# Weight split pieces queued behind every copy and split of the attention steps, value blocks ahead of prompt values, and other step lists for pairs 1, 6 and 7

## The chip, the cores and the metric

The kernel runs on one core of a Trainium2 chip. The metric is the device time of one execution in microseconds (us). The core has a matrix engine (PE, with its weight loads shown apart as PEld), a vector engine (DVE), a scalar engine (ACT), a general engine (POOL), and queues that issue DMAs (SP's above all). Each works through its own list of instructions in order and waits at semaphores for the others.

## The reference

The program is one inference step of a small trunk of two layers, on 512 frames of a new stream (the prompt) and 16 new frames each of 8 running streams (the sample), 640 columns in all, with 1024 features. Layer 0 is a convolution module and a feed-forward part (FFN). Layer 1 is the attention, with 16 heads of 64, and a second FFN. Everything is float32. The attention, where the change lies, is this (cut):

```python
k, v = jnp.split(rms_norm(h, norm_kv) @ w_kv, 2, axis=-1)
q = rms_norm(h, norm_attn[j]) @ w_q[j]
# prompt: each chunk of 64 frames sees itself and up to 8 chunks before it
s = jnp.einsum("bqhd,bkhd->bhqk", q_blk, k_blk) * scale + bias
p = jax.nn.softmax(jnp.where(valid, s, NEG_INF), axis=-1)
o = jnp.einsum("bhqk,bkhd->bqhd", p, v_blk)
# sample: 16 new frames see 512 cached rows and themselves, then the same softmax
h = h + o @ w_o[j]
```

## The kernel before

Every matrix product keeps float32 accuracy by splitting both factors into a high and a low part (`hi` a rounded copy made on ACT, `lo = x - hi` made on DVE) and adding three products: hi·hi, lo·hi, hi·lo. A weight set of 128x2048 comes by one DMA into `raw` and is split piece by piece into `whi` (ACT) and `wlo` (DVE). There are two buffers of each, so a set's pieces can be written once PE is done with the set two before it.

The attention stage works on **eight pairs of heads**, p = 0 to 7. For each pair the string `BO[p]` (L66 to L68) is a list of steps that sets PE's order by hand:

- `A`: the scores of the two prompt heads (`heads`, L1395, 24 matmuls that read `KH`, `KL`, `QH`, `QL`, into two wide PSUM tiles `w` and two narrow ones `am`), then bias and maximum on DVE (L1202), exponentials on ACT (L1194), scaling on DVE (L1428).
- `s0`, `s1`: the scores of the sample in two halves, into wide PSUM tiles, with their own maximum (`Sn`, `Ss`, L1202).
- `b00` to `b12`: transposes of the prompt's scores (L1441), copied to `PT` by ACT (L1445) or DVE (L1447).
- `t0`, `t1`: transposes of the sample's scores (L1491), copied to `PTs` by ACT (L1502); `n0`, `n1`: one more transpose each (L1497), copied to `PM` and `PN` by DVE (L1499).
- `P`: the prompt's values (`pair_c`, 16 matmuls, L1457); its result is split into `ohi` (ACT, L190) and `olo` (DVE, L192).
- `c0`, `c1`: the sample's values, 40 matmuls each (L1513); DVE scales each result (L1518). `d0`, `d1`: their transposes (L1522), split into `ohi` and `olo` in two parts each.
- `f` and a number: that many **fills**, or `f*`, all that the pair has left.

The `am` tiles have two buffers that are handed round in the order of the steps, so every `b`, `t`, `n`, `P`, `c` and `d` writes the buffer that the step but one before it used, and waits until that one's copy has been taken.

A **fill** is a portion of a projection (L1268) that is independent of the pair at work: one third of a product of the next keys and queries (`k`), of values (`v`), or one product of the attention's output projection (`o`). `SETS` lists the weight sets in order and `FILL[p]` how many fills a pair has. The keys and queries of pair p+1 are made by fills of pair p; a copy on ACT and a subtraction on DVE then turn them into `KH`, `KL`, `QH`, `QL` (`heads_split`, L1392 and L1393). An `o` fill ends in an addition to the residual `h` on DVE (L1357); after `s1` it uses half of a wide tile `w` where it can, and two products are then added at once.

While one weight set is used, the pieces of the next are issued, some at each fill (`pieces`, L1271). Where they stand in the lists of ACT and DVE is set by `past[-LAG]`: a piece is put behind the last **noted** instruction on each engine as it was four steps or fills ago (`note` records them in `ahead`). Noted are the copies to `PT`, the exponentials, the scalings, the `K`/`Q` splits and the additions that end fills; not noted are the copies to `PTs`, `PM` and `PN`, the scaling after `c`, and the splits after `P` and `d`.

After pair 7 a last projection (`halves`, L1527, matmuls at L202 to L204, additions at L1544) adds the rest of the attention to `h`; its weights are split whole (128x2048, L178 on ACT, L183 on DVE). The squares for the next norm follow (L1612), with the first weights of the second FFN (split at L374 and L375).

Of the kernel before, what the change touches and what calls it, by code (L numbers as in the profile page):

```python
# [8 lines left out]
F32 = mybir.dt.float32  # L9
# [55 lines left out]
          13 23 42 63 33"""  # L65
BO = ["A f4 s0 s1 f3 b00 f1 b01 f1 b02 f1 b10 f1 b11 f1 b12 f1 t0 f1 t1 f1 n0 n1 f1 P c0 c1 f2 d0 f1 d1 f*"] * 8  # L66
BO[1] = BO[6] = "A f4 s0 s1 f2 b00 f1 b01 b02 f1 b10 b11 f1 b12 t0 f1 t1 n0 n1 f1 P c0 c1 f1 d0 d1 f*"
BO[7] = "A f2 s0 s1 f4 b00 f1 b01 b02 f1 b10 b11 f1 b12 t0 f1 t1 n0 n1 f1 P c0 c1 f* d0 d1"  # L68
FILL = 27, 12, 28, 27, 28, 27, 16, 12
SETS = "k1 v1 k2 k3 o0 k4 v2 k5 o1 k6 v3 k7 o2"  # L70
LAG = 4
SSQ1 = 'aaaaaaaa'
# [13 lines left out]
def tile_trunk(ctx, tc, xT, vecs, hist, w_pw1, w_pw2, w_in0, w_out0, w_os0, w_in1, w_out1, w_os1,  # L86
# [102 lines left out]
    def xsplit(src, hi, lo):  # L189
        split_end[0] = nc.scalar.activation(out=hi, in_=src, func=AF.Copy).ins  # L190
        norm_end["xh"].append(split_end[0])
        nc.vector.tensor_tensor(out=lo, in0=src, in1=hi.bitcast(F32), op=ALU.subtract)  # L192

# [1012 lines left out]
    fill, step_end, spare_w2 = None, [None], [None, []]  # L1206
    ahead, past = {}, [{}] * LAG

    def note(ins):
        ahead[ins.ins.engine] = ins.ins  # L1210
        return ins

    def proj_kq(p):
# [126 lines left out]
    def set_o(r, w):  # L1340
        wh, wl = w
        for g0 in (0, NH):
            for m in range(KT):
                if spare_w2[0] and m % 2 == 0:
                    spare_w2[1] = [w2t().rearrange("p (a n) -> p a n", a=2)]
# [103 lines left out]
    def pair_c(p, PTs):  # L1449
        VT = vts[p // 2]  # L1450
        po = amt()
        for k in range(4):
            n = (4 - k) * P
            for hh in range(2):
                r = slice(hh * DH, hh * DH + DH)
                v0 = (p % 2) * P + hh * DH
                step_end[0] = nc.tensor.matmul(  # L1457
                    po[r, k * P:512], VT[:, 1 + k, v0:v0 + DH],
                    PTs[hh][:, POFF[k]:POFF[k] + n], start=(k == 0), stop=(k == 3)).ins
        xsplit(po, oT[p][0][:, P:], oT[p][1][:, P:])  # L1460

# [25 lines left out]
    def samp_b(u, S):  # L1487
# [7 lines left out]
        def rest():  # L1495
            tn = amt()
            step_end[0] = nc.tensor.transpose(tn[:, 0:P], S[:, 512 - v0:640 - v0], ident).ins  # L1497
            pn = PN if u else ap.tile([P, P], F32, tag="PM", name=nm("PM"), bufs=1)
            nc.vector.tensor_copy(pn[v0:, :], tn[v0:, 0:P])  # L1499
            return PT, pn  # L1500

        nc.scalar.activation(out=PT, in_=tr, func=AF.Copy)  # L1502
        return rest

    def samp_c(p, u, PTs, S, rs, VC):
# [4 lines left out]
        for k in range(5):  # L1510
            for b in range(4):
# [4 lines left out]
                    else VT[:, 0, (p % 2) * P:(p % 2) * P + P], start=k == 0, stop=k == 4).ins  # L1516
        os_ = S[:, 0:P]
        nc.vector.tensor_scalar(out=os_, in0=pv[:, 0:P], scalar1=rs[:, 0:1], scalar2=None,  # L1518
                                op0=ALU.mult)
        def rest():  # L1520
# [3 lines left out]
            for hh in range(2):  # L1524
                r = slice(hh * DH, hh * DH + DH)
                xsplit(trv[r, :, hh, :],
                       oT[p][0][r, v0:v0 + 64].rearrange("p (b q) -> p b q", q=SB),  # L1527
# [27 lines left out]
    for p in range(NP):  # L1555
# [3 lines left out]
        else:  # L1559
            oT[p] = (op_.tile([P, NT], F32, tag="kt", name=nm("ohi"), bufs=2).bitcast(F32R),  # L1560
                     op_.tile([P, NT], F32, tag="qt", name=nm("olo"), bufs=QB).bitcast(F32R))
        ha, sa, pt, ps, left = {}, {}, {}, {}, FILL[p]
        cache = [samp_load(p, u) for u in range(2)]
        for op in BO[p].split():
            if op[0] == "f":
                n = left if op[1] == "*" else min(left, int(op[1]))
                left -= n
                for _ in range(n):
                    with pe():
                        next(fill)  # L1570
                    past.append(dict(ahead))
                continue
# [258 lines left out]
```

## Time and profile before

| | |
|---|---|
| time, median of 3 runs (lowest to highest) | 1471.48 us (1471.44 to 1471.75) |
| the profiled execution: its own time, and its span | 1473.27 us, 1471.5 us |
| mean granted clock of PE | 0.992 |
| attention stage with all pairs, 693.5 to 1014.6 us | 321.1 us |
| busy in it: PE, DVE, ACT, POOL | 304.2, 190.9, 144.1, 46.4 us |

In rows of the profile, an instruction stands as line, engine, operation, what it writes, "<-", what it reads, and its shape. Behind an instruction, "[1.87 <-ACT PTs L1502]" says that its engine sat idle for 1.87 us before it, until ACT had written PTs at line 1502. Times at the left of a row are us from the start of the span; the time behind them is how long the row's instructions ran, several of one kind being merged ("x16").

### The profile page before, as it was taken

The numbers are of one execution on the slowest core, as the hardware profiler recorded it, in microseconds if no ns is written. First come the engines' busy times: TensorE is split into PE (matmuls) and PEld (weight loads), VectorE is DVE, ScalarE is ACT, GpSimd is POOL, SyncE is SP. The second block draws the span as 40 slices with busy tenths as digits, with TensorE's granted clock in tenths as the row PEclk, the third lists the DMA queues.
The fourth block names the chain that finished last, engine by engine and source line by source line (L and its number), as shares of the span: only waits on it lengthen the run. The fifth ranks groups of instructions, "written<-read, shape, count | busy, mean of one in ns | idle before, by whom it ended". The sixth has DMA issues, their size and how long they took to land. (4 is left out here: it accounts for less than half of the span.)

```text
span 1471.5 us, 28237 instructions
## 1 busy us (share of the span) xinstructions
PE 1433.5 (97%) x11086; PEld 1372.4 (93%) x11086; DVE 1117.9 (76%) x2486; ACT 748.9 (51%) x1633; POOL 282.3 (19%) x335
## 2 busy tenths in 40 slices
PE   9999999999999999999999999988999999999998
PEld 8998799999999999999877897877998999999998
DVE  6789867989788888666565656566899888888855
ACT  5666554554554554454544453433554455455443
POOL 5689120011110111012111111011001111111101
PEclk9999999999999999999999999999999999999999
DMA  7267434054544544415564464551224544544522
GB/s 241 77 180 184 120 86 143 18 136 142 136 105 146 134 105 132 125 58 207 183 205 152 143 208 149 164 185 37 79 76 130 140 119 119 150 118 107 157 63 72
DMA packets 66933, 192.58 MB, mean 131 GB/s; under 512 B 12144, under 2 KB 30320, under 8 KB 58480
## 3 DMA queue, kind: packets, MB, share of 16 engines
q1 hardware_dynamic: 52432, 160.58, 33.8%
q0 software_dynamic: 13504, 29.37, 10.0%
q8 instruction: 87, 1.43, 0.4%
q10 hardware_dynamic: 864, 0.83, 0.2%
q14 instruction: 46, 0.38, 0.1%
HBM read 179.14 MB, written 11.61 MB: 130 GB/s over the span
## 5 line engine op out<-in xcount | busy, mean ns | idle before, releaser
L442 PE MATMUL mm<-XH,whi 128*128 128x320 f32 x896 | 275.7, 310 | 2.6 <-ACT t L454 2.6
L442 PE MATMUL mm<-XH,wlo 128*128 128x320 f32 x896 | 276.1, 309 | 0.0
L442 PE MATMUL mm<-XL,whi 128*128 128x320 f32 x896 | 274.5, 309 | 0.0
L374 ACT ACTIVATE whi<-raw 128x512 fp32r<-128x512 f32 (+2 forms) x280 | 168.7, 613 | 142.3 <-PE mm L442 109.9
L375 DVE TENSOR_TENSOR wlo<-raw,whi 128x512 fp32r<-128x512 f32 (+2 forms) x280 | 185.4, 671 | 20.3 <-ACT whi L374 18.9
L442 PE MATMUL mm<-hid,whi 128*128 128x320 f32 x732 | 171.4, 310 | 2.7 <-DVE hid L375 2.3
L442 PEld LDWEIGHTS mm<-XH,whi 128*128 128x128 f32 x896 | 167.7, 188 | 4.2 <-ACT t L454 4.2
L442 PEld LDWEIGHTS mm<-XH,wlo 128*128 128x128 f32 x896 | 168.1, 188 | 0.0
L442 PEld LDWEIGHTS mm<-XL,whi 128*128 128x128 f32 x896 | 167.7, 188 | 0.0
L202 PE MATMUL mm<-xh,whi 128*128 128x320 f32 (+2 forms) x416 | 129.4, 313 | 0.8 <-DVE h L705 0.4
L442 PEld LDWEIGHTS mm<-hid,whi 128*128 128x128 f32 x732 | 124.8, 188 | 4.9 <-DVE hid L375 3.3
L203 PE MATMUL mm<-xh,wlo 128*128 128x320 f32 (+2 forms) x416 | 128.1, 310 | 0.0
L204 PE MATMUL mm<-xl,whi 128*128 128x320 f32 (+2 forms) x416 | 126.0, 310 | 0.0
L442 PE MATMUL mm<-hid,wlo 128*128 128x320 f32 x366 | 113.0, 309 | 0.0
L442 PE MATMUL mm<-XH,shi 128*128 128x320 f32 x344 | 105.9, 309 | 0.7 <-DVE h L1544 0.7
L442 PE MATMUL mm<-XH,slo 128*128 128x320 f32 x344 | 106.0, 308 | 0.0
L442 PE MATMUL mm<-XL,shi 128*128 128x320 f32 x344 | 105.5, 308 | 0.0
L844 POOL TENSOR_TENSOR ca<-ca,cvt 128x512 f32<-128x512 f32 x60 | 91.8, 1531 | 17.9 <-ACT cvt L841 11.3
L420 POOL DMA_DIRECT2D s<-in_w_in x38 | 22.0, 580 | 381.6 <-DVE wlo L375 150.6
L374 ACT ACTIVATE shi<-raw 128x512 fp32r<-128x512 f32 (+1 forms) x114 | 66.8, 588 | 43.0 <-PE mm L442 39.2
L583 DVE TENSOR_TENSOR h<-h,mm 128x320 f32<-128x320 f32 x168 | 80.5, 485 | 5.8 <-PE mm L442 5.6
L454 ACT ACTIVATE t<-mm 128x320 f32<-128x320 f32 x114 | 49.6, 435 | 66.0 <-PE mm L442 65.8
(331 smaller groups left out, 3728.6 us busy)
## 6 DMA issues: line engine op xcount, KB each, us to landing
raw<-in_w_in SPq DMA_DIRECT2D x38, 1024.0 KB
s<-in_w_in POOLq DMA_DIRECT2D x76, 256.0 KB, 4.1
raw<-in_w_os SPq DMA_DIRECT2D x24, 768.0 KB
cache<-in_ck SPq DMA_DIRECT2D x32, 512.0 KB
cache<-in_cv SPq DMA_DIRECT2D x32, 512.0 KB
raw<-in_w_pw SPq DMA_DIRECT2D x11, 1024.0 KB
s<-in_w_os POOLq DMA_DIRECT2D x48, 192.0 KB, 3.6
raw<-in_w_kq SPq DMA_DIRECT2D x8, 1024.0 KB
```

The source lines that it names most:

```text
L202: nc.tensor.matmul(ps, wh, xh, start=(first and i == 0), stop=False)
L203: nc.tensor.matmul(ps, wl, xh, start=False, stop=False)
L204: end = nc.tensor.matmul(ps, wh, xl, start=False, stop=(stop and i == last))
L374: put_end[1] = nc.scalar.activation(out=hi, in_=src, func=AF.Copy).ins
L375: put_end[0] = nc.vector.tensor_tensor(out=lo, in0=src, in1=hi.bitcast(F32), op=sub).ins
L420: nc.gpsimd.dma_start(s1, src[:, 2 * n:3 * n])
L442: last = nc.tensor.matmul(pt, wt, v, start=(first and k == i == 0), stop=(k == n - 1 and i == 2), skip_group_check=True)
L454: keeps.append(nc.scalar.activation(out=t, in_=pt, func=AF.Copy).ins)
L583: nc.vector.tensor_tensor(out=hv, in0=hv, in1=pt, op=sub if row else add)
L844: nc.gpsimd.tensor_tensor(out=acc, in0=acc, in1=pr, op=ALU.add)
```

## The change

Four things change, all in the attention stage.

- `LAG` goes from 4 to 1, and the copies to `PTs`, `PM`, `PN`, the scaling after `c`, and both halves of every split of `P` and `d` (the new helper `osplit`) are noted too. A weight piece thus stands behind everything that the last step put on its engine.
- In every list `c0 c1` now stand ahead of `P`. In pairs 0 and 2 to 5 a fill goes between `n0` and `n1` as well, and one fill fewer behind `P`.
- Pairs 1 and 6, which have 12 fills each now, end in `f1 n0 n1 c0 c1 P d0 d1` with no fill left; pair 7 has five fills behind `s1`, `P` behind `c1`, and its last fills between and behind `d0` and `d1`. `FILL` moves four `o` fills from pair 6 to pair 7.
- The last two `o` fills of a pair use the small `mm` tiles instead of a wide one (`left[0] > 2`), so that two additions of 128x320 take the place of one of 128x640.

```diff
-BO = ["A f4 s0 s1 f3 b00 f1 b01 f1 b02 f1 b10 f1 b11 f1 b12 f1 t0 f1 t1 f1 n0 n1 f1 P c0 c1 f2 d0 f1 d1 f*"] * 8
-BO[1] = BO[6] = "A f4 s0 s1 f2 b00 f1 b01 b02 f1 b10 b11 f1 b12 t0 f1 t1 n0 n1 f1 P c0 c1 f1 d0 d1 f*"
-BO[7] = "A f2 s0 s1 f4 b00 f1 b01 b02 f1 b10 b11 f1 b12 t0 f1 t1 n0 n1 f1 P c0 c1 f* d0 d1"
-FILL = 27, 12, 28, 27, 28, 27, 16, 12
+BO = ["A f4 s0 s1 f3 b00 f1 b01 f1 b02 f1 b10 f1 b11 f1 b12 f1 t0 f1 t1 f1 n0 f1 n1 f1 c0 c1 P f1 d0 f1 d1 f*"] * 8
+BO[1] = BO[6] = "A f4 s0 s1 f3 b00 f1 b01 b02 f1 b10 f1 b11 b12 f1 t0 t1 f1 n0 n1 c0 c1 P d0 d1 f*"
+BO[7] = "A f2 s0 s1 f5 b00 f1 b01 b02 f1 b10 f1 b11 b12 f1 t0 f1 t1 n0 n1 f1 c0 c1 P d0 f1 d1 f*"
+FILL = 27, 12, 28, 27, 28, 27, 12, 16
-LAG = 4
+LAG = 1
...
-        nc.vector.tensor_tensor(out=lo, in0=src, in1=hi.bitcast(F32), op=ALU.subtract)
+        return nc.vector.tensor_tensor(out=lo, in0=src, in1=hi.bitcast(F32), op=ALU.subtract)
...
+    def osplit(src, hi, lo):
+        note(xsplit(src, hi, lo))
+        ahead[split_end[0].engine] = split_end[0]
...
-                if spare_w2[0] and m % 2 == 0:
+                if spare_w2[0] and m % 2 == 0 and left[0] > 2:
...
-        xsplit(po, oT[p][0][:, P:], oT[p][1][:, P:])
+        osplit(po, oT[p][0][:, P:], oT[p][1][:, P:])
...
-            nc.vector.tensor_copy(pn[v0:, :], tn[v0:, 0:P])
+            note(nc.vector.tensor_copy(pn[v0:, :], tn[v0:, 0:P]))
...
-        nc.scalar.activation(out=PT, in_=tr, func=AF.Copy)
+        note(nc.scalar.activation(out=PT, in_=tr, func=AF.Copy))
...
-        nc.vector.tensor_scalar(out=os_, in0=pv[:, 0:P], scalar1=rs[:, 0:1], scalar2=None,
-                                op0=ALU.mult)
+        note(nc.vector.tensor_scalar(out=os_, in0=pv[:, 0:P], scalar1=rs[:, 0:1], scalar2=None,
+                                     op0=ALU.mult))
...
-                xsplit(trv[r, :, hh, :],
+                osplit(trv[r, :, hh, :],
...
-                n = left if op[1] == "*" else min(left, int(op[1]))
-                left -= n
-                for _ in range(n):
+                for _ in range(left[0] if op[1] == "*" else min(left[0], int(op[1]))):
                     with pe():
                         next(fill)
+                    left[0] -= 1
                     past.append(dict(ahead))
```

Three places show what the scheduler makes of it. The first is ACT's list in pair 2, from the copy of the prompt's transposes (`PT`) to the split behind `P` (`ohi` 128x512); `whi` is the set of keys and queries that is split in pieces. Before:

```order
L1392 ACTIVATE KH_9179<-kt_8967 128x512
L1445 ACTIVATE PT_8966<-am_9148 128x512
L1286 ACTIVATE whi_9199<-raw_9198,vec 128x128
L1392 ACTIVATE QH_9181<-qt_8968 128x512
L1286 ACTIVATE whi_9199<-raw_9198,vec 128x128 x13
L1502 ACTIVATE PTs_9209<-am_9204 128x512
L1286 ACTIVATE whi_9199<-raw_9198,vec 128x128 x2
L1502 ACTIVATE PTs_9225<-am_9220 128x512
L190 ACTIVATE ohi_8881<-am_9252 128x512
```

The same stretch of ACT's list in the changed kernel:

```order
L1396 ACTIVATE KH_9179<-kt_8967 128x512
L1449 ACTIVATE PT_8966<-am_9148 128x512
L1396 ACTIVATE QH_9181<-qt_8968 128x512
L1290 ACTIVATE whi_9199<-raw_9198,vec 128x128 x2
L1506 ACTIVATE PTs_9209<-am_9204 128x512
L1290 ACTIVATE whi_9199<-raw_9198,vec 128x128
L1506 ACTIVATE PTs_9225<-am_9220 128x512
L1290 ACTIVATE whi_9199<-raw_9198,vec 128x128 x3
L190 ACTIVATE ohi_8881<-am_9305 128x512
```

Two pieces instead of thirteen stand between `QH` and the first copy to `PTs`; the others have gone behind it, among and behind the splits of `P` and `d`. Pair 4 has the same.

The second place is DVE's list at the end of pair 6, where the weights of the last projection are split whole (`wlo` 128x2048). Before:

```order
L1499 COPY PM_11404<-am_11402 128x128
L1499 COPY PN<-am_11406 64x128
L192 TENSOR_TENSOR olo_11106<-am_11420,ohi_11105 128x512
L1518 TENSOR_SCALAR Sn<-am_11431,rs_11254 128x128
L1518 TENSOR_SCALAR Ss_11265<-am_11453,rs_11272 128x128
L1306 TENSOR_TENSOR qt_11192<-mm_11383,bc_7500 128x384
L1357 TENSOR_TENSOR h<-w_1323_11503,h 128x2x320
L183 TENSOR_TENSOR wlo_11860<-raw_11858,whi_11859 128x2048
L192 TENSOR_TENSOR olo_11106<-am_11491,ohi_11105 64x64
L192 TENSOR_TENSOR olo_11106<-am_11497,ohi_11105 64x64
L1393 TENSOR_TENSOR QL_11486<-qt_11192,QH_11485 128x512
L1357 TENSOR_TENSOR h<-w_1324_11517,h 128x2x320
```

The same stretch of DVE's list in the changed kernel:

```order
L1310 TENSOR_TENSOR qt_11196<-mm_11370,bc_7500 128x384
L1503 COPY PM_11435<-am_11433 128x128
L1503 COPY PN<-am_11437 64x128
L183 TENSOR_TENSOR wlo_11866<-raw_11864,whi_11865 128x2048
L1397 TENSOR_TENSOR QL_11428<-qt_11196,QH_11427 128x512
L1522 TENSOR_SCALAR Sn<-am_11440,rs_11258 128x128
L1522 TENSOR_SCALAR Ss_11269<-am_11462,rs_11276 128x128
L192 TENSOR_TENSOR olo_11110<-am_11484,ohi_11109 128x512
L192 TENSOR_TENSOR olo_11110<-am_11495,ohi_11109 64x64 x2
L192 TENSOR_TENSOR olo_11110<-am_11501,ohi_11109 64x64 x2
```

The whole subtraction has moved from behind the scaling after `c` to ahead of it, `qt` has moved ahead of `PM`, and no addition to `h` stands there any more. On ACT the whole copy to `whi` stands behind the two copies to `PTs` and ahead of `QH`.

The third place is ACT's list at the end of pair 7, with the splits behind `P` and `d` (`ohi`) and the first weights of the second FFN (`whi` 128x1024 and `shi`). Before:

```order
L1502 ACTIVATE PTs_11768<-am_11763 128x512
L190 ACTIVATE ohi_11531<-am_11784 128x512
L374 ACTIVATE whi_12057<-raw_12174 128x1024 x2
L190 ACTIVATE ohi_11531<-am_11846 64x64
L190 ACTIVATE ohi_11531<-am_11852 64x64
L190 ACTIVATE ohi_11531<-am_11846 64x64
L190 ACTIVATE ohi_11531<-am_11852 64x64
L374 ACTIVATE shi_12061<-raw_12103 128x512
```

The same stretch of ACT's list in the changed kernel:

```order
L1506 ACTIVATE PTs_11758<-am_11753 128x512
L190 ACTIVATE ohi_11507<-am_11818 128x512
L190 ACTIVATE ohi_11507<-am_11829 64x64 x2
L190 ACTIVATE ohi_11507<-am_11842 64x64 x2
L374 ACTIVATE shi_12067<-raw_12109 128x512
L374 ACTIVATE shi_12071<-raw_12109 128x512
L374 ACTIVATE shi_12069<-raw_12109 128x512
L374 ACTIVATE hid_12110<-raw_12109 128x512
L374 ACTIVATE whi_12063<-raw_12180 128x1024 x2
```

The two large copies have gone from ahead of the splits of `d` to behind them and behind the four smaller ones. At the beginning of pair 7, DVE's list has changed too: the maxima of the sample's scores (`Sn`, `Ss`) stand behind two additions to `h` and ahead of the scaling of the first head's scores, where they stood behind that scaling before. Outside the attention stage and the projection behind it (`halves`), the lists of all engines keep their order.

More of the change, by code (lines that the diff above doesn't have):

```diff
@@ L1206, in tile_trunk @@
     fill, step_end, spare_w2 = None, [None], [None, []]
-    ahead, past = {}, [{}] * LAG
+    ahead, past, left = {}, [{}] * LAG, [0]
     def note(ins):
@@ L1561, in tile_trunk @@
                      op_.tile([P, NT], F32, tag="qt", name=nm("olo"), bufs=QB).bitcast(F32R))
-        ha, sa, pt, ps, left = {}, {}, {}, {}, FILL[p]
+        ha, sa, pt, ps, left[0] = {}, {}, {}, {}, FILL[p]
         cache = [samp_load(p, u) for u in range(2)]
```

## The prediction

> **What bounds the kernel now.** I read the busy times first, then PE's waits, then the granted clock in windows of the attention stage, then PE, ACT and DVE side by side around each pause.
>
> The page, with the span and the busy time of each engine (us, share, instructions):
>
> ```profile
> span 1471.5 us, 28237 instructions
> PE 1433.5 (97%) x11086; PEld 1372.4 (93%) x11086; DVE 1117.9 (76%) x2486; ACT 748.9 (51%) x1633; POOL 282.3 (19%) x335
> ```
>
> PE is the bound: it works 97% of the span, and the change removes none of its matmuls. What can be won is PE's idle time and the time that it runs at a lower clock. PE's waits (line and tile <- what released it: us in total, times, longest) say where in the attention stage the idle time lies:
>
> ```profile
> PE am L1497 <- ACT PTs L1502: 4.3, 3, 1.9
> PE w L1412 <- DVE h L1357: 3.5, 3, 2.5
> ...
> PE mm L202 <- ACT ohi L190: 2.6, 1, 2.6
> ...
> PE w L1268 <- DVE mx L1202: 1.9, 1, 1.9
> ...
> PE am L1513 <- DVE olo L192: 1.6, 8, 0.3
> PE am L1497 <- DVE PM L1499: 1.5, 4, 0.4
> ...
> PE w L1412 <- ACT QH L1392: 1.1, 1, 1.1
> ```
>
> These seven rows hold 16.5 us. None of them names the pieces `whi` or `wlo` of a weight set, so weights arrive in time today.
>
> A pause costs more than itself when the clock falls after it. The windows (us; busy PE, PEld, DVE, ACT, POOL; then the granted clock PEclk, the DMA share and GB/s):
>
> ```profile
> 766.72:770.14 3.42, 2.10 (x20) 1.48 (x19) 2.85 (x9) 2.42 (x8) 0.00 (x0) 1.00 0.94 334
> 794.03:797.44 3.41, 1.78 (x10) 1.28 (x12) 0.80 (x3) 2.25 (x7) 0.00 (x0) 1.00 0.00 0
> 797.44:800.86 3.42, 3.42 (x14) 1.34 (x12) 1.40 (x4) 0.00 (x0) 0.00 (x0) 0.50 0.00 0
> 882.78:886.19 3.41, 1.74 (x10) 1.28 (x12) 0.76 (x3) 2.29 (x7) 0.00 (x0) 1.00 0.01 2
> 978.35:981.76 3.41, 0.90 (x7) 0.54 (x8) 3.10 (x7) 0.35 (x2) 0.00 (x0) 1.00 0.71 220
> 992.00:995.42 3.42, 3.42 (x14) 3.42 (x14) 2.06 (x11) 1.63 (x4) 1.24 (x2) 0.50 0.28 41
> 1014.60:1027.05 12.45, 11.47 (x67) 11.21 (x67) 10.14 (x25) 5.80 (x12) 0.00 (x0) 0.86 0.01 1
> 693.51:1014.60 321.09, 304.22 (x2824) 266.27 (x2823) 190.87 (x606) 144.10 (x413) 46.42 (x81) 0.98 0.52 166
> ```
>
> In 794.03 to 797.44 PE is busy for 1.78 us, and in the 3.42 us behind it the granted clock is 0.50: half of 3.42, 1.7 us of work, is lost. The windows from 882.78 (1.74 busy) and 978.35 (0.90) stand ahead of two more half-clock stretches. The one from 766.72, with 2.10 busy, was followed by none. So a stretch at half clock comes, in this trace, where PE was busy for about 1.8 us or less of 3.4. The whole attention stage lasts 321.09 us with PE busy 304.22: 17 us is the most that pauses alone can give there.
>
> **Pairs 2 and 4: the pieces ahead of `PTs`.** ACT's timeline (start, us, what it did) and PE's:
>
> ```profile
> 790.84 3.89 ACT L1286 ACTIVATE whi<-raw,vec 128x128 fp32r<-128x128 f32 x13
> ```
>
> PE beside it, in pair 2:
>
> ```profile
> 795.27 0.33 PE L1497 MATMUL am<-ident,Sn 128*128 128x128 f32 x1 [1.87 <-ACT PTs L1502]
> ...
> 797.12 4.07 PE L1457 MATMUL am<-PT,vt 128*64 128x512 f32 x16
> ```
>
> and `P` of pair 1, at full clock:
>
> ```profile
> 760.38 2.38 PE L1457 MATMUL am<-PT,vt 128*64 128x512 f32 x16
> ```
>
> Thirteen pieces take 3.89 us, 0.30 each, and `n0` waits 1.87 us for the copy behind them. With two pieces there (0.6 us), the copy comes 11 x 0.30 = 3.3 us sooner, so that wait goes. What is late next is `n1`, which waited 0.38 (the row on `PM` with four waits and 0.4 the longest); the fill now between `n0` and `n1` covers it. So 2.25 us in each of the two pairs: **4.5**. The 4.07 of `P` against 2.38 in pair 1 is the half clock: 1.7 each, **3.4**. In pairs 1 and 6 the other two of the four waits on `PM` go as well, **0.7**, as a fill separates `t1` from `n0`.
>
> **The copies and splits between steps.** PE's timeline at pair 1's end and at the scores (`A`) of pairs 2 and 3, and ACT's split of `P`:
>
> ```profile
> 764.17 1.08 PE L1513 MATMUL am<-cache,PTs 128*32 128x128 f32 x32 [0.19 <-DVE olo L192]
> ...
> 768.03 0.50 PE L1412 MATMUL w<-KH,QH 64*128 64x512 f32 x2 [1.09 <-ACT QH L1392]
> ...
> 771.01 0.38 PE L1268 MATMUL mm<-xh,whi 128*128 128x256 f32 x1
> ```
>
> PE at `A` of pair 3:
>
> ```profile
> 815.80 0.50 PE L1412 MATMUL w<-KH,QH 64*128 64x512 f32 x1 [0.48 <-DVE h L1357]
> ...
> 817.93 0.39 PE L1268 MATMUL mm<-xh,whi 128*128 128x256 f32 x1
> ```
>
> ACT behind `P` of pair 1:
>
> ```profile
> 762.80 0.60 ACT L190 ACTIVATE ohi<-am 128x512 fp32r<-128x512 f32 x1 [4.14 <-PE am L1457]
> ```
>
> - `c1` waited for `P`'s split in all eight pairs, 1.6 by its row. With `c0 c1` ahead of `P` it doesn't: **1.6**.
> - `A` of pair 2 starts 1.09 late and takes 771.01 - 768.03 = 2.98, where `A` of pair 3 takes 817.93 - 815.80 = 2.13. Pair 1's queries are now finished five steps sooner, so 1.09 + 0.85 = **1.9** goes.
> - `A` of pairs 3 and 5 wait 0.48 each for a 640-wide addition to `h`. The last two additions are now of single tiles and no longer hold a wide one: **1.0**.
>
> Against these stands what the lists of pairs 1 and 6 add. DVE around the end of pair 6:
>
> ```profile
> 965.92 0.29 DVE L1499 COPY PM<-am 128x128 f32<-128x128 f32 x1 [0.84 <-PE am L1497]
> ...
> 974.49 0.56 DVE L1306 TENSOR_TENSOR qt<-mm,bc 128x384 f32<-128x384 f32 x1 [0.86 <-PE mm L1268]
> ...
> 977.21 2.28 DVE L183 TENSOR_TENSOR wlo<-raw,whi 128x2048 fp32r<-128x2048 f32 x1
> ...
> 979.67 0.68 DVE L1393 TENSOR_TENSOR QL<-qt,QH 128x512 fp32r<-128x512 f32 x1
> 980.27 0.81 DVE L1357 TENSOR_TENSOR h<-w,h 128x640 f32<-128x640 f32 x1
> ```
>
> ACT there:
>
> ```profile
> 974.48 1.91 ACT L178 ACTIVATE whi<-raw 128x2048 fp32r<-128x2048 f32 x1 [3.36 <-PE mm L1268]
> ```
>
> - `c0` writes the `am` buffer of `n0` and waits until `PM` is copied. The fill just ahead of `n0` is the last of the queries, and its `qt` (0.56) now stands ahead of `PM` (0.29) on DVE: 0.85 in each of pairs 1 and 6, **1.7** added. No bound is below zero, since nothing is taken away there; if `qt` starts a fill earlier than I think, it is 0.
> - `d1` writes the buffer of `P`, and only `d0`, two transposes, stands between them. In pair 1 of before, `P` ended at 760.38 + 2.38 = 762.76, `ohi` followed at 762.80, and the waiting `c1` started at 764.17: 1.4 us. Less 0.1 for `d0` that is 1.3, twice: **2.6** added. The cover that is gone is `c0`.
> - In pair 6 `P` writes `c0`'s buffer, and so waits for the scaling of `c0`. On DVE `PM`, `PN`, the 2.28 of `wlo` and the 0.68 of `QL` stand ahead of that scaling, and `wlo` needs `whi`, which takes 1.91 on ACT from the second `PTs` on. From there DVE is free after 1.91 + 2.28 + 0.68 + 0.3 = 5.2 us, while PE has `n0`, `n1`, `c0` and `c1`, about 0.8 + 2 x 1.1 = 3.0: it waits **2.2**. By the windows above such a gap halves the clock, 1.7 more: **3.9** added. Behind the waiting `P` stand `d0`, `d1` and `A` of pair 7. Its ends: 0, if the copy to `whi` finds ACT free much sooner, and 5.2.
>
> **Pair 7 and the end.** PE's waits:
>
> ```profile
> 981.13 0.50 PE L1412 MATMUL w<-KH,QH 64*128 64x512 f32 x1 [2.51 <-DVE h L1357]
> ...
> 984.44 0.63 PE L1268 MATMUL mm<-ohi,whi 128*128 128x320 f32 x1
> ...
> 991.80 0.48 PE L1268 MATMUL w<-ohi,whi 128*128 128x320 f32 x1 [1.87 <-DVE mx L1202]
> ...
> 1014.60 0.42 PE L202 MATMUL mm<-ohi,whi 128*128 128x320 f32 x1 [2.61 <-ACT ohi L190]
> ```
>
> DVE ahead of the fill at 991.80, and ACT ahead of the end:
>
> ```profile
> 989.80 1.27 DVE L1428 TENSOR_SCALAR S<-S,rs 128x512 f32<-128x512 f32 x4
> 990.99 0.75 DVE L1202 CUSTOM_DVE_ANT_0 Sn<-w,BS 128x576 f32<-128x576 f32 x1
> ```
> ```profile
> 1011.80 2.00 ACT L374 ACTIVATE whi<-raw 128x1024 fp32r<-128x1024 f32 x2 [3.25 <-PE w L1268]
> ```
>
> - `A` waited 2.51 for an addition (980.27) that stood behind `wlo`, and took 3.31 instead of 2.13 at the lower clock. No addition is left there: 2.51 + 1.18 = **3.7** goes.
> - The first wide fill behind `s1` waited 1.87 for the sample's maximum, and the window from 992.00 ran at half clock. The maximum has moved ahead of the scaling (1.27), which leaves 0.6, but behind two additions of at most 0.81 each: 0.6 to 2.2, of which I take **1.2**, as one addition has time to finish beside `s1`. Then 1.87 + 1.7 = **3.6** goes and 1.2 comes back.
> - At the end the two copies of 2.00 us stood ahead of `ohi`, and PE waited 2.61. They now stand behind it. The window from 1014.60 lost (1 - 0.86) x 12.45 = 1.7 by the clock, but DVE was busy 10.14 of its 12.45, so I count 1.2 of it: 2.61 + 1.2 = **3.8** goes.
> - `d1` and the finer alternation of fills and steps in pair 7 and the other lists: **1.0** added, between 0 and 2, by the 0.29 of such a copy a few times.
>
> **The weights.** Every piece now stands later, and LAG 1 gives it the last place that is possible. I cost that at nothing. Its cover is a whole weight set: pieces are issued while the set before is used, and no wait row names one now. The rival below says what it costs without the cover.
>
> **The sum.** Removed: 4.5 + 3.4 + 0.7 + 1.6 + 1.9 + 1.0 + 3.7 + 3.6 + 3.8 = 24.2. Added: 1.7 + 2.6 + 3.9 + 1.2 + 1.0 = 10.4. Net 13.8 faster. The sum is made against the span of 1471.5; the profiled execution's own time, 1473.27, has 1.8 us around the span, and the median without a profile, 1471.48, happens to equal the span, so I take the sum off that: **1457.7 us**.
>
> The Trainium skill, "TensorE: Matmul & The Clock Gate", section "Why this matters for your kernels", weighs a clock loss only for idle gaps longer than about 3 us. The trace differs: a 1.87 us gap, in a window with 1.78 us of work, was followed by a clock of 0.50. By the page, the wait of pair 6 would cost no clock.
>
> **The rivals.**
>
> - *The waits return elsewhere, with the clock.* The pauses that I price without the clock in pairs 1, 6 and 7 (0.85 and 1.3 us close together, 1.2 in pair 7) each fill a window with under 1.8 us of work, three more stretches of 1.7: 5.1 back, **1462.8**. For it: 1.87 us was enough. Against it: the window from 766.72 with 2.10 busy was not. Chance 0.23.
> - *The new waits are hidden.* The copy to `whi` in pair 6 may start sooner and `qt` be done: 1.7 + 3.9 + 2.6 of the added terms fall away, **1449.5**. Against it: the buffers follow the order strictly. Chance 0.13.
> - *A gap of 2.2 us doesn't halve the clock.* Pair 6 then costs 2.2, and the time is **1456.0**. Against it: the window from 794.03. Chance 0.04. (This is what the rule of the Trainium skill's "TensorE: Matmul & The Clock Gate" would give; on the gaps that this trace shows, it doesn't hold.)
> - *Slower: weights come late.* Where a set ends, PE waits for the next set's last piece: 0.30 on ACT, 0.36 on DVE for the low part (by 2.28 to 1.91), and a copy of 0.6 ahead of it make 1.25, and the half clock 1.7 more: 2.9 at each of 12 set borders, 35 us, **1493**. It decides against the change from 13.8 / 12 = 1.15 us a border. Against it: no wait row names a piece today, and the order shows most of a set's pieces well ahead of its first use. Chance 0.05.
> - *Nothing comes of it.* The pauses may be set by something that the moved rows only hide, such as the transfers of the caches. Against it: ACT's rows end exactly where PE's waits do. Chance 0.05, at **1471**.
>
> **How the numbers follow.** The forecast, 1453 to 1462, has 0.50. The range takes in the hidden waits and the returned ones: 1448 to 1466, which leaves out the two cases at the end and the edges, under 2 in 10. A measurement of this kernel can tell about 0.2% (2.9 us) from no change. Faster: 0.50 + 0.23 + 0.13 + 0.04, and a little for a weaker form of late weights, 0.91; slower 0.05; the same 0.04.
>
> **What would show it.** Right: no row of `n0` waiting for `PTs` in pairs 2 and 4; `P` of pairs 2 to 5 at 2.4 us; `c1` without waits on `olo`; `A` of pair 7 at once; `ohi` at the end ahead of the copies for the FFN; in pair 6 a wait of `P` for the scaling of `c0` of about 2.2 us, with one stretch at half clock; pauses of 1.3 at `d1` of pairs 1 and 6. Wrong: PE waits that name `whi` or `wlo`; half-clock stretches in pairs 1, 6 and 7 beyond that one; a wide fill of pair 7 that still waits 2 us.

## The result, and the profile after

| | before | changed |
|---|---|---|
| time, median (lowest to highest) | 1471.62 us (1471.44 to 1472.6, 4 runs) | 1452.14 us (1451.49 to 1454.72, 4 runs) |
| ratio to before | | 0.987, 95% interval 0.9852 to 0.9887 |
| the profiled execution's own time | 1473.27 us | 1452.18 us |
| its mean granted clock | 0.992 | 0.999 |

The changed kernel is 19.5 us faster, 1.3%. The forecast was 13.8 us faster, 1457.7, in a range from 1448 to 1466.

The page of the changed kernel, its span and its busy times:

```profile
span 1450.3 us, 28244 instructions
PE 1420.6 (98%) x11086; PEld 1365.9 (94%) x11086; DVE 1119.6 (77%) x2489; ACT 749.7 (52%) x1633; POOL 283.0 (20%) x335
```

PE has the same 11086 matmuls and is busy 12.9 us less. At most 8.5 of this comes from the clock in the attention stage (the windows below); part of the rest is matmuls that ran alone ahead of a wait and counted as busy there (the rows under "What a wait costs"), which no run sizes as a whole. DVE and ACT do what they did. PE's waits in the stages that the change touches (line and tile <- releaser: us in total, times, longest):

```profile
PE am L1526 <- DVE olo L192: 2.7, 3, 1.2
PE am L1461 <- DVE Sn L1522: 2.1, 1, 2.1
...
PE am L1517 <- DVE PM L1503: 1.2, 2, 0.6
PE w L1622 <- DVE sqs L1615: 1.0, 1, 1.0
...
PE w L1272 <- DVE mx L1202: 0.8, 1, 0.8
...
PE am L1501 <- ACT PTs L1506: 0.6, 1, 0.6
```

Of the seven rows shown of before (16.5 us) two are left, `mx` with 0.8 for 1.9 and `PTs` with 0.6 for 4.3. Three have come in their place, and each is one that the prediction adds: `d1` for the split of `P` (L1526), `P` of pair 6 for the scaling of `c0` (L1461), and `c0` for `PM` (L1517). The wait for `sqs` was there before, with the same 1.0.

To see where the time went, the attention stage is cut at each pair's first matmul of the scores, from PE's timeline, and ended at the first product of the second FFN. Each entry is the difference of two such starts, in us:

| from A of pair | before | changed | difference |
|---|---|---|---|
| 0 to A of pair 1 | 44.77 | 44.27 | -0.5 |
| 1 to 2 | 29.74 | 29.49 | -0.3 |
| 2 to 3 | 46.79 | 41.20 | -5.6 |
| 3 to 4 | 42.90 | 41.42 | -1.5 |
| 4 to 5 | 45.90 | 41.17 | -4.7 |
| 5 to 6 | 42.90 | 41.42 | -1.5 |
| 6 to 7 (four fills fewer now) | 31.60 | 31.25 | -0.4 |
| 7 to the FFN (four more) | 54.50 | 46.71 | -7.8 |

Together 339.1 against 316.9, 22.2 us less. The windows of the whole stage, of before (us; busy PE, PEld, DVE, ACT, POOL; granted clock, DMA share, GB/s):

```profile
693.51:1032.62 339.11, 320.99 (x2925) 282.34 (x2924) 205.95 (x637) 150.85 (x427) 48.15 (x82) 0.97 0.50 161
```

and of the changed kernel:

```profile
694.92:1011.84 316.92, 308.24 (x2925) 276.26 (x2925) 207.53 (x640) 151.54 (x427) 48.19 (x82) 1.00 0.53 172
```

The granted clock went from 0.97 to 1.00: before, five stretches of 3.41 us at 0.50 lay in it, which cost at most 5 x 1.7 = 8.5 us of PE's work; now there is none. The other 13.7 us or more are waits, counted from one start to the next. The stage moved by 22.2 and the profiled execution by 1473.27 - 1452.18 = 21.1, because the changed kernel reached the stage 1.4 us later in it; single executions of one kernel differ by more (1451.49 to 1454.72 here).

In pair 2 the thirteen pieces ahead of `PTs` have become two. ACT's timeline there in the changed kernel:

```profile
790.62 0.68 ACT L1290 ACTIVATE whi<-raw,vec 128x128 fp32r<-128x128 f32 x2
791.21 0.58 ACT L1506 ACTIVATE PTs<-am 128x512 f32<-128x512 f32 x1
...
792.33 0.60 ACT L1506 ACTIVATE PTs<-am 128x512 f32<-128x512 f32 x1 [0.26 <-PE am L1495]
```

PE beside it:

```profile
793.02 0.27 PE L1501 MATMUL am<-ident,Sn 128*128 128x128 f32 x1
794.00 0.27 PE L1501 MATMUL am<-ident,Ss 128*128 128x128 f32 x1
795.08 1.08 PE L1517 MATMUL am<-cache,PTs 128*32 128x128 f32 x32
...
797.40 2.37 PE L1461 MATMUL am<-PT,vt 128*64 128x512 f32 x15
```

The second copy to `PTs` now waits for PE, and PE no longer waits for the copies; `n0`, `n1` and `c0` show no idle time, and `P` takes 2.37 where it took 4.07.

At the end of pair 6 the waits forecast have come. DVE's timeline:

```profile
955.80 0.56 DVE L1310 TENSOR_TENSOR qt<-mm,bc 128x384 f32<-128x384 f32 x1 [2.36 <-PE mm L1272]
956.28 0.28 DVE L1503 COPY PM<-am 128x128 f32<-128x128 f32 x1
...
957.75 2.29 DVE L183 TENSOR_TENSOR wlo<-raw,whi 128x2048 fp32r<-128x2048 f32 x1 [0.86 <-ACT whi L178]
959.96 0.69 DVE L1397 TENSOR_TENSOR QL<-qt,QH 128x512 fp32r<-128x512 f32 x1
960.67 0.35 DVE L1522 TENSOR_SCALAR Sn<-am,rs 128x128 f32<-128x128 f32 x1
```

PE's:

```profile
956.61 1.08 PE L1517 MATMUL am<-cache,PTs 128*32 128x128 f32 x32 [0.63 <-DVE PM L1503]
...
961.08 2.37 PE L1461 MATMUL am<-PT,vt 128*64 128x512 f32 x16 [2.08 <-DVE Sn L1522]
963.38 0.33 PE L1526 MATMUL am<-ident,Sn 128*128 128x128 f32 x1
964.88 0.33 PE L1526 MATMUL am<-ident,Ss 128*128 128x128 f32 x1 [1.16 <-DVE olo L192]
```

`c0` waits behind `qt` and `PM`, `P` behind `wlo` and `QL`, and `d1` for the split of `P`, one after the other as they stand in the lists. But `P` takes 2.37: no half clock follows.

### The profile page after: what moved, and what is told of

Its sections match the earlier page's. It is cut to its first block, busy times and chain, and to the rows that moved or that the text cites. A ratio compares the mean times of both kernels' runs of the same rounds, so it can differ in the third digit from the quotient of the medians.

```text
span 1450.3 us, 28244 instructions
## 1 busy us (share of the span) xinstructions
PE 1420.6 (98%) x11086; PEld 1365.9 (94%) x11086; DVE 1119.6 (77%) x2489; ACT 749.7 (52%) x1633; POOL 283.0 (20%) x335
## 3 DMA queue, kind: packets, MB, share of 16 engines
q0 software_dynamic: 13504, 29.37, 10.2%
## 5 line engine op out<-in xcount | busy, mean ns | idle before, releaser
L844 POOL TENSOR_TENSOR ca<-ca,cvt 128x512 f32<-128x512 f32 x60 | 92.0, 1533 | 17.7 <-ACT cvt L841 11.2
```

What stands on the lines that cost most here:

```text
L844: nc.gpsimd.tensor_tensor(out=acc, in0=acc, in1=pr, op=ALU.add)
```

## The experiments

The runs of the kernel before that are named with a job's medians were taken on the same chip as that job's kernels.

**One half at a time.** The pieces alone: the changed kernel with the lists (`BO`), `FILL` and tiles of before, so that only the place of the pieces is new.

```diff
-FILL = 27, 12, 28, 27, 28, 27, 12, 16
+FILL = 27, 12, 28, 27, 28, 27, 16, 12
...
-                if spare_w2[0] and m % 2 == 0 and left[0] > 2:
+                if spare_w2[0] and m % 2 == 0:
```

> Only the place of the weight pieces changes (LAG 1 and the added notes); lists, FILL and the tiles of the last fills are those of before. Theory (the parts add up): n0 of pairs 2 and 4 no longer waits for PTs, 2 x 2.6 us by start to start, and P there runs at full clock, 2 x 1.7: about 8.6 us less, 1463; the waits of c1 on olo (8 x 0.2), of A in pairs 3, 5 and 7 and the 2.6 us at the end stay. Rival (the pieces' gain needs the new lists, since pieces now stand ahead of the split of P or of d): c1 or d waits longer than before in pairs 2 and 4, and under 4 us is left, 1467.5 or more.

The lists alone: the changed kernel with `LAG` and the noted instructions of before.

```diff
-LAG = 1
+LAG = 4
...
-        osplit(po, oT[p][0][:, P:], oT[p][1][:, P:])
+        xsplit(po, oT[p][0][:, P:], oT[p][1][:, P:])
...
-        note(nc.scalar.activation(out=PT, in_=tr, func=AF.Copy))
+        nc.scalar.activation(out=PT, in_=tr, func=AF.Copy)
```

> The new lists, FILL and the tiles of the last fills, with LAG 4 and without the added notes. Theory (the parts add up): the 8.6 us of pairs 2 and 4 are missing from the changed kernel's gain of 19.5, so 1460 to 1461; n0 of pairs 2 and 4 waits about 1.9 us for PTs behind 13 pieces, with a half-clock stretch behind it, while c1 has no waits on olo and the end has ohi ahead of the FFN copies. Rival (lists alone let pieces stand ahead of P's split as well): over 1464.

Measured beside 1472.23 for the kernel before: pieces alone 1462.09 (ratio 0.9938, interval 0.9914 to 0.9961), lists alone 1461.76 (0.9933, 0.9919 to 0.9948), both changes 1450.61 in the same job (0.9856, 0.9841 to 0.9871). The halves give 10.1 and 10.5, together 20.6, and the whole 21.6: in sum the parts add up. With the pieces alone, pairs 2 and 4 last 42.04 and 41.50 us instead of 46.79 and 45.90. The other pairs keep their times within 0.2, but for two: the stretch from pair 7 to the FFN lasts 52.61 instead of 54.50, and pair 3 lasts 43.76 instead of 42.90 because a transpose waits for `PT` behind pieces that now stand later:

```profile
827.68 0.44 PE L1445 MATMUL am<-ident,S 128*128 128x128 f32 x2 [0.63 <-ACT PT L1449]
```

That price is absent in the whole change, whose list has other fills there.

Place by place the halves do not add up so simply. With the lists alone, pairs 2 and 4 last 3.5 and 2.0 us longer than in the changed kernel, 5.6 together where 8.6 was expected, and the stretch from pair 7 to the FFN lasts 52.37 instead of 46.71, 5.7 longer, which neither expected text has. With the lists alone, DVE's list has the first head's scaling ahead of the sample's maximum again, and PE waits for that maximum, with two windows at half clock behind it:

```profile
981.16 0.64 PE L1272 MATMUL w<-ohi,whi 128*128 128x320 f32 x1 [3.79 <-DVE mx L1202]
```

So about half of what the pieces add to the lists is won in pair 7, by another order of DVE's list, and not at `PTs`.

The lists alone showed something else, too. Pair 2 lasts 44.71 us there and pair 4 only 43.21, with the same pieces ahead of the same copy. Windows of that kernel, each pair's pause and the 3.41 us behind it:

```profile
792.42:795.83 3.41, 1.54 (x13) 1.28 (x11) 1.29 (x4) 3.41 (x12) 0.00 (x0) 1.00 0.04 13
795.83:799.24 3.41, 3.41 (x18) 3.04 (x20) 2.02 (x5) 0.69 (x2) 0.00 (x0) 0.50 0.00 0
877.75:881.16 3.41, 2.00 (x15) 1.73 (x13) 2.06 (x6) 3.41 (x13) 0.00 (x0) 1.00 0.10 35
881.16:884.58 3.42, 2.96 (x46) 2.76 (x50) 1.94 (x5) 1.47 (x4) 0.00 (x0) 1.00 0.00 0
```

In pair 2 the pause fell into one window, with 1.54 busy, and half clock followed. In pair 4 it fell across two, with 2.00 and 2.96 busy, and none followed. The half-clock stretches of every execution lie on a grid of 3.41 us, and where the grid lies against the program differs between executions. So one and the same pause costs up to 1.7 us more or doesn't, by chance; here the pairs differ by 44.71 - 43.21 = 1.5.

**Does the wait of `P` in pair 6 lower the clock?** The changed kernel, again:

> The changed kernel unaltered, for another execution in the profile. Theory (the clock is granted anew on a grid of 3.41 us that is fixed within one execution and differs from one to the next; a window with under about 1.8 us of PE work is followed by one at 0.50): the wait of P in pair 6, 2.1 us long, is again there, and a stretch at 0.50 follows in this profile if, and only if, one window of this execution's grid holds 1.6 us or more of PE's idle time there; single times scatter between 1451.5 and 1455. Rival (a gap of 2.1 us never lowers the clock): no stretch in the attention stage in any execution, times within 0.5 us.

It ran at 1450.61 (1450.11 to 1451.61), with the same wait of 2.08 and no stretch at half clock in the attention stage. Its grid cut the pause in two (PE was still busy 1.97 us in the emptier window), so this alone tells nothing. It was looked at again in the last job:

> The changed kernel unaltered once more, beside the next one: 1450 to 1453, and the attention stage, from A of pair 0 to the first product of the second FFN, at 316.9 us if the wait of P in pair 6 is followed by no stretch at half clock, 318.6 if it is.

It ran at 1451.51 (1451.23 to 1452.43), beside 1471.1 for the kernel before, the stage at 316.9 once more. Here the grid did hold the pause. Windows of this execution, the pause and what follows:

```profile
959.00:962.42 3.42, 1.52 (x8) 0.63 (x10) 2.07 (x4) 0.00 (x0) 0.00 (x0) 1.00 0.87 280
962.42:965.83 3.41, 2.25 (x20) 1.45 (x18) 1.27 (x5) 1.35 (x5) 0.00 (x0) 1.00 0.90 297
```

With 1.52 us busy, less than in pair 2 of before (1.78), no half clock follows. The condition that I expected, that PE's busy time in a window of the grid decides, failed here; the experiment below without `left[0] > 2` holds another such window. The matmuls that fill the window differ: here it is half of `P`, there products of fills and two transposes. Two experiments further down have windows that fit no bound on busy time either: the first two lines are the kernel before with `c0 c1` ahead of `P`, where 1.76 us, all of it products of the last projection, keep the clock; the last two are the weights of the last projection in pieces, where 2.33 us, with six one-column products of the squares among them, lose it:

```profile
1004.83:1008.24 3.41, 1.76 (x12) 1.76 (x13) 0.71 (x4) 3.21 (x9) 0.00 (x0) 1.00 0.00 0
1008.24:1011.65 3.41, 3.41 (x25) 3.41 (x24) 3.40 (x8) 2.23 (x5) 0.00 (x0) 1.00 0.02 5
1001.89:1005.31 3.42, 2.33 (x18) 2.14 (x17) 3.10 (x8) 0.00 (x0) 0.96 (x1) 1.00 0.16 19
1005.31:1008.72 3.41, 3.41 (x15) 3.10 (x14) 2.39 (x5) 0.44 (x1) 0.77 (x1) 0.50 0.99 334
```

So the pause was made longer. First the scaling of `c0` was done five times over:

```diff
+        if p == 6 and not u:
+            for _ in range(4):
+                nc.vector.tensor_scalar(out=os_, in0=pv[:, 0:P], scalar1=rs[:, 0:1], scalar2=None,
+                                        op0=ALU.mult)
```

> The scaling of c0 in pair 6 is done five times over instead of once, so that P waits 4 x 0.3 = 1.2 us longer, 3.3 us in all. Grid theory: however the grid lies, a window now holds over 1.6 us of idle time, so a stretch at 0.50 follows always: 1.2 + 1.7 = 2.9 us over the changed kernel's undisturbed executions (1452.1), 1455. Rival (the clock has nothing to do with it): 1.2 us more, 1453.3.

This missed: `P` waited 2.33 instead of 2.08, since it was released by the scaling of `c1`, which stood second among the scalings, and the time was 1451.56 (1450.47 to 1453.76). Nothing about the clock follows from it. With both scalings repeated (`if p == 6:`), eight more in all:

> The scalings of c0 and of c1 in pair 6 are each done five times over, eight more scalings of 0.27 us in turn, so that P waits some 2.2 us longer, 4.3 in all. Grid theory: however the 3.41 us grid lies, one window holds over 2.1 us of this idle time, so a stretch at 0.50 follows always: pair 6 and what follows it last 2.2 + 1.7 = 3.9 us longer than in the changed kernel. Rival (such a gap doesn't lower the clock): 2.2 us longer.

It took 1460.65 (1460.06 to 1463.24). PE's timeline there, and further on in pair 7:

```profile
963.46 4.53 PE L1461 MATMUL am<-PT,vt 128*64 128x512 f32 x16 [4.23 <-DVE Sn L1526]
...
981.17 0.64 PE L1272 MATMUL w<-ohi,whi 128*128 128x320 f32 x1 [3.79 <-DVE mx L1202]
```

The windows of that stretch:

```profile
959.13:962.54 3.41, 0.10 (x4) 0.00 (x0) 3.38 (x9) 0.00 (x0) 0.00 (x0) 1.00 0.92 291
962.54:965.96 3.42, 2.50 (x8) 0.98 (x10) 1.03 (x4) 0.00 (x0) 0.00 (x0) 0.50 0.93 344
965.96:969.37 3.41, 2.44 (x13) 1.11 (x9) 0.71 (x2) 0.70 (x2) 0.00 (x0) 0.50 0.69 276
969.37:972.78 3.41, 3.38 (x21) 2.86 (x21) 0.77 (x4) 0.65 (x3) 0.00 (x0) 0.50 0.00 0
976.20:979.61 3.41, 1.18 (x28) 0.41 (x20) 1.82 (x9) 2.98 (x11) 0.00 (x0) 1.00 0.51 161
979.61:983.02 3.41, 1.85 (x7) 1.85 (x8) 3.40 (x14) 2.36 (x9) 0.42 (x1) 0.50 0.00 0
983.02:986.44 3.42, 3.42 (x15) 3.42 (x14) 1.21 (x5) 0.87 (x2) 0.88 (x2) 0.50 0.51 153
```

The pause is 4.23, 2.15 longer, a window of the grid is empty but for 0.10, and half clock follows, as the grid theory had it. But it lasts three windows, not one: at half clock PE is busy 2.50 and 2.44 us of 3.41, with short waits between, and that doesn't bring the clock back. From pair 6 to the FFN the kernel lasts 35.70 + 53.46 = 89.2 us against 78.0, 11.2 more, where 3.9 was expected. So the run with 2.15 us more of pause has 9 us more behind it, some of it by a second pause of 3.79 in pair 7, with two more windows at half clock: DVE's list has the sample's maximum behind the scaling of the first head's scores there, and ahead of it in the changed kernel. The lists alone have the same order and the same 3.79 without any added scaling. So the 11.2 is not the clock's alone, and the run doesn't say what the pause by itself costs; what it shows is the half clock right behind it.

The Trainium skill, "TensorE: Matmul & The Clock Gate", section "Why this matters for your kernels", warns of idle gaps over about 3 us. Here the gap of 4.23 lowered the clock and five gaps of 2.08 in pair 6 did not (three executions of the changed kernel, the lists alone, and the kernel without `left[0] > 2`; one window held the pause in two of the five), which agrees; the gaps of 1.87 with 0.38 behind them in pairs 2 and 4 lowered it where the grid held them, which doesn't.

**What a wait costs.** Wide tiles for the last two fills again:

```diff
-                if spare_w2[0] and m % 2 == 0 and left[0] > 2:
+                if spare_w2[0] and m % 2 == 0:
```

> The changed kernel with wide tiles for the last two o fills of a pair as before. Start-to-start theory (a wait costs PE more than its idle time: the first matmuls behind it run at a wider pitch): A of pairs 3 and 5 waits 0.48 us for h again, and pairs 3 and 5 last 0.85 us longer each: 1.7 us more than the changed kernel. Rival (idle time is the whole cost, as the prediction summed it): 0.48 each, 1.0 more.

Measured 1455.86 (1454.02 to 1459.67) beside 1471.67 for before. `A` of pairs 3 and 5 waits 0.5 for `h` again, and those pairs last 43.07 and 42.39 us, 1.65 and 0.97 more than in the changed kernel, so 2.6 in all. Pair 3 has another new wait of 0.46, for `PT`, so pair 5 with its 0.97 is the clean one, and the start-to-start theory is nearer. The end changed too: DVE's additions come later, the squares are waited for 2.2 us instead of 1.0, with two windows at half clock, and the stretch from pair 7 to the FFN lasts 49.97 instead of 46.71. The rows show why the idle time is not the whole cost. `A` of pair 3 in the kernel before, and in the changed one:

```profile
814.82 0.50 PE L1412 MATMUL w<-KH,QH 64*128 64x512 f32 x1
815.80 0.50 PE L1412 MATMUL w<-KH,QH 64*128 64x512 f32 x1 [0.48 <-DVE h L1357]
809.88 0.50 PE L1416 MATMUL w<-KH,QH 64*128 64x512 f32 x2
```

The first two matmuls of `A` start together in the changed kernel, in one row. Before, the second started 0.98 us after the first: the 0.50 that the first one runs counts as busy, and only the 0.48 behind it as idle. So the hidden part lies mainly ahead of the idle time, in a matmul that otherwise overlaps with the next one, and not in a wider pitch behind it, as the expected text has it.

The kernel before with the value blocks ahead of `P`, and nothing else:

```diff
-... n0 n1 f1 P c0 c1 ...
+... n0 n1 f1 c0 c1 P ...
```

> The kernel before with c0 c1 ahead of P in every list, and nothing else. Start-to-start theory: c1 loses its waits on olo, and each pair 0 to 5 lasts 0.37 to 0.5 us less, about 3 us in all eight pairs, 1468.5. Rival (idle time is the whole cost): 0.2 in each pair, 1.6 in all.

Measured 1466.54 (ratio 0.9967, 0.9957 to 0.9977) beside 1471.1, 4.6 less and more than either expected. The total decides nothing: its profiled execution has three half-clock stretches fewer in the stage than that of the kernel before, and pair 6 lasts 1.34 longer, as `A` of pair 7 now waits 1.39 for an addition to `h`. The pairs decide: pairs 0, 1, 3 and 5, which have no stretch at half clock in either kernel, last 0.41, 0.41, 0.42 and 0.45 less. In the trace the first matmul of `c1` starts 0.47 behind the last of `c0` with the wait, and 0.09 without it at full clock: 0.27 in which that last matmul runs, and 0.20 of idle time. So a wait of 0.20 in the list of waits is worth twice that here, 3.1 to 3.4 us over eight pairs, because it leaves a matmul of 0.27 standing alone.

**Can the new waits be had for less?** The weights of the last projection as a last set of pieces beside pair 7's fills:

```diff
-        todo = [(t[0], int(t[1])) for t in SETS.split()]
+        todo = [(t[0], int(t[1])) for t in SETS.split()] + [("o", 3)]
...
-        for i, (kind, r) in enumerate(todo):
+        for i, (kind, r) in enumerate(todo[:-1]):
...
+        last_w.extend(cur[0])
...
-        wh, wl = wsplit(w_o[r], 16, P)
+        wh, wl = last_w
```

> The weights of the last projection come in eight pieces beside pair 7's fills instead of whole at the end of pair 6. Theory (P of pair 6 waits only because 1.9 us of whi and 2.3 us of wlo stand ahead of the scaling): its wait of 2.1 us goes, QL comes sooner, and the pieces hide beside pair 7's fills: 2.1 us less than the changed kernel, 1448 to 1450. Rival (the split's 4.2 us only move, to where ACT and DVE are waited for in pair 7): n1, the wide fill and the transposes of pair 7 wait longer, no gain within 0.5 us.

Two more fills in pairs 1 and 6:

```diff
-BO[1] = BO[6] = "... t0 t1 f1 n0 n1 c0 c1 P d0 d1 f*"
+BO[1] = BO[6] = "... t0 t1 f1 n0 n1 f1 c0 c1 P d0 f1 d1"
-FILL = 27, 12, 28, 27, 28, 27, 12, 16
+FILL = 27, 14, 26, 27, 28, 27, 14, 14
```

> The changed kernel with two more fills in pairs 1 and 6, one ahead of c0 and one between d0 and d1, taken from pairs 2 and 7 (FILL 27, 14, 26, 27, 28, 27, 14, 14). Theory (PM and the split of P are waited for because no fill covers them): the waits of 0.6 at c0 and 1.2 at d1 go in pairs 1 and 6, by start to start 0.85 + 1.35 each, 4.4 us, and the wait of P in pair 6 shrinks by one fill, about 0.9; at the end no fill is left behind d1 of pair 7, and the last projection waits about 1.2 for its split: 4 us less than the changed kernel, about 1447.5. Rival (the fills move the waits, since pieces of the next set now stand ahead of the splits): within 1 us of the changed kernel.

Both of them:

> Both of the two edits above. Theory: the gains add, less what the shorter wait of P in pair 6 counts twice: 5 us less than the changed kernel, about 1446.5. Rival: no better than the better one of the two.

Measured beside 1471.67: pieces for the last projection 1450.32 (ratio 0.9851, 0.9836 to 0.9865), more fills 1449.68 (0.9847, 0.9833 to 0.9862), both 1447.39 (0.9832, 0.9816 to 0.9848). The changed kernel did not run in this job. Against its ratios of 0.9856 to 0.987, neither edit alone is clear of the noise, and their stages last 317.0 and 316.5 us, against its 316.9; both together are clear of it, with a stage of 314.3. With the pieces the wait of `P` is gone and pair 6 lasts 29.10 us instead of 31.25, as the theory had it; from pair 7 to the FFN it lasts 48.95 instead of 46.71, of which 1.7 is one stretch at half clock that followed the wait for the squares. With the fills, pairs 1 and 2 together last 69.14 instead of 70.69, and pair 6 about as long as in the changed kernel with two fills more in it, though the wait of `P` there fell only from 2.08 to 1.78; the end pays 1.1 for the split of `d1`, as expected, and 0.6 more for the squares and a stretch at half clock behind them, which were not. So each theory got its place right and its sum too high.

> The kernel with both edits again, to be compared with the changed kernel on the same chip: theory (the waits of pairs 1 and 6 are gone and nothing replaces them but 1.1 us at the end) 3 to 5 us less than the changed kernel; rival (the earlier difference was one of executions) within 1 us.

Measured 1448.04 (1445.42 to 1449.74; ratio to before 0.9842, 0.9824 to 0.9861) beside 1451.51 for the changed kernel in the same job: 3.5 us less, within the 3 to 5. The intervals of the two ratios overlap, but the stages agree on where it comes from: pairs 1 and 2 last 68.92 instead of 70.66 and pair 6 29.28 instead of 31.25, 3.7 less, and what follows 1.8 more, with one stretch at half clock in it. That is a net of 1.9 in the two profiled executions; the 3.5 is of the medians.

## Why the prediction was right, and where its sizes were off

The direction, the range and all mechanisms but one held; the gain was 5.7 us larger than the forecast, by errors that nearly all point the same way. So the range held in part by its width, and a time inside it says little about the single terms.

- **Pieces ahead of `PTs`** (4.5 + 3.4): right. Moving them alone gave 10.1 us; pairs 2 and 4 became 4.75 and 4.4 us shorter, 9.2 against 7.9 forecast, 1.3 more. The other part of the 10.1 is 1.9 in pair 7, less 0.9 in pair 3; that the pieces also change DVE's order in pair 7 (5.7 us beside the new lists) is not in the forecast's terms for them.
- **`c1` behind the split of `P`** (1.6): the mechanism was right, the size was not. The experiment with that order alone gave 0.41 to 0.45 in each of the undisturbed pairs, 3.1 to 3.4 for eight: 1.5 to 1.8 too small, as the sum took the idle time for the whole cost.
- **`A` of pairs 3 and 5** (1.0): the same. Putting the wide tiles back cost pair 5 0.97 instead of 0.48, and pair 3 more by another wait: 1.0 too small for the two. The prediction reads `A` of pair 3 as 817.93 - 815.80 = 2.13, from its second matmul on; the first started at 814.82, so it took 3.11. The 0.85 that it took from 2.13 for pair 2 stands all the same, by luck: an `A` without waits lasts 2.12 in the changed kernel.
- **The half clock behind the wait of `P` in pair 6** (1.7 of the 3.9): did not come, in any of the executions of the changed kernel whose profile was taken, though its wait of 2.08 was within 0.15 of the forecast. This is the step that failed: "By the windows above such a gap halves the clock". Windows with 1.78 and 1.74 busy had done so, and I took the busy time for the condition. The execution with 1.52 busy shows that it is not enough.
- **The other added waits**: 2.6 at `d1` of pairs 1 and 6 (measured 1.16 idle each), 1.7 at `c0` (0.63 each), 1.2 at the wide fill of pair 7 (0.75): right in place. The forecast priced these by distances between starts, and by these they came to size: in pair 6 `d1` starts 1.49 us behind `d0`, `c0` 0.90 behind `n1` and `P` 2.35 behind the last matmul of `c1`; in pair 7 the wide fill starts 0.97 behind the last matmul of `s1`.
- **Pair 7 and the end** (3.7 + 3.6 + 3.8): `A` of pair 7 and the last projection start without their waits of 2.5 and 2.6, and the half-clock stretches behind them are gone. From pair 7 to the FFN, with four fills more, the stage is 7.8 us shorter. Of the three half-clock stretches there, at most 5.1 us, the forecast counted 1.2 + 1.7 + 1.2; and `A` of pair 7 had its second matmul 3.0 us behind its first (978.12 and 981.13), of which the idle row has 2.51.

By place, the table has pairs 0 to 5 at 14.0 us less, where the terms of the forecast make 10.2; the first three points cover this 3.8. Pairs 6 and 7 together are 8.1 less against 3.6; of these 4.5, 1.7 is the half clock that did not come, and the mis-sized terms of pair 7 and of `c1` make about 1.9 more. No run separates the rest. That is 8.4 missed between the two profiled executions of the stage, against 5.7 between the medians: the executions compared differ in the parts outside the stage and in their chance of half-clock stretches. Two of the rivals named the direction of the error: "a gap of 2.2 us doesn't halve the clock", at 1456.0 with a chance of 0.04, was what happened in pair 6, and the hidden waits, at 1449.5, came nearer to the time than the forecast, though for another reason, as the waits were not hidden. Late weight pieces did not appear: no PE wait of the changed kernel names `whi` or `wlo` in the stage.

Open is what decides whether the clock is lowered. The 3.41 us grid and the empty window of the longest pause are shown; that windows with 1.52 us of `P` and with 1.76 us of products keep the clock, and one with 1.54 us of fills and a transpose and one with 2.33 us that holds the squares' products lose it, is shown and not explained. Whether it is the kind of matmul that counts was not tried.

## What to carry to other kernels

A wait that a queue's order makes on the engine that bounds the kernel costs more than its idle time, by what the last matmul ahead of it runs and would have shared with the next (0.2 to 0.5 us here, twice the cost of a short wait), and it may bring a stretch at half clock of up to 1.7 us besides; price such waits by the distance from one start to the next, in the same place with and without the wait. Put work that nobody is waiting for behind the copies that free a buffer, and look in every queue at what the moved step then stands behind: here that saved 10 us in pieces, while the new step order, which alone has the same wait of 2.08 in pair 6, put a whole weight split ahead of one scaling, and cutting it into pieces, with two more fills, won 3.5 more.

## What the runs showed of the hardware

- The stretches at a granted clock of 0.50 start on a grid of 3.41 us that keeps its place through an execution and has another place in the next. The same pause was followed by one in pair 2 and not in pair 4 of one execution, 1.5 us apart. Executions of one kernel scatter by 1.2 to 5.7 us between the lowest and the highest, and this can make a part of it.
- At half clock a window that is not full keeps it there: after the 4.23 us pause, windows with 2.50 and 2.44 us busy were followed by half clock again, three in a row. In all runs, apart from the stretch that ends most executions, the five windows at half clock with 1.85 to 2.65 us busy were followed by half again, and those with 3.38 or more by full, but for one with 3.38 in the kernel without `left[0] > 2`.
- Busy time in a window, by the trace, doesn't fully decide: 1.52 us of `P` and 1.76 us of projection products were followed by full clock, 1.54 us in the lists-alone kernel and 2.33 us with the squares' products by half.
- A matmul ahead of a wait runs alone, and its running time counts as busy: 0.27 us ahead of `c1`, beside 0.20 idle, where starts are 0.09 apart without the wait; 0.50 us in `A` of pair 3, beside 0.48 idle.
